# A decoder block with hybrid attention on one core: wait counts, the place of four weight chunks in the stream, and the shape of two row operations are changed

## The chip, the cores and the metric

The kernel runs on one core of one Trainium2 chip. The metric is device time in microseconds (us) of one execution, the median of several runs. The engines are named as the profile names them: PE is TensorE (matmuls; PEld its weight loads), DVE is VectorE, ACT is ScalarE, POOL is GpSimd and SP is SyncE, which here only issues DMAs. Each engine works through its own instructions in the order in which the program issues them. The program does not reorder them: the schedule is written by hand.

## The reference

One layer of a decoder block, batch 1, 256 tokens, model width 1024, float32. Cut to what matters:

```python
h = x @ w_in                                   # q, k, v, z, gates, NSA q and three k/v pairs
q, k, v = silu(causal_dwconv([dq, dk, dv]))    # 8 heads of 128, q and k l2-normalised
g = cumsum(log decay per chunk of 64)          # gated delta rule:
lower = strict_tril(k_beta @ k.T * decay)
u, w = triangular_solve(I + lower, [v_beta, k_beta * exp(g)])
for each chunk: v_new = u - w @ S; out = q_dec @ S + qk @ v_new; S = S * g_last + k_dec.T @ v_new
y_dn  = rmsnorm(out) * silu(z)
y_nsa = gates * (compressed + selected-block + window attention)   # 8 heads, 2 kv heads, rotary
y = sig(mg_dn) * (y_dn @ W_dn) + sig(mg_nsa) * (y_nsa @ W_nsa)
x = LN(alpha * x + y @ W_out)
x = LN(alpha * x + conv_glu(x))                # up (2 x 2816), causal conv of 3, silu gate, down
```

The output is x, 256 x 1024.

## The kernel before, in words

**The weight stream.** All big weights are cut into chunks of 128 x 1024 values. `plan()` (L66) writes the order in which they are stored and used: the input projection (k, q, kc, vc, nq, ksl, kwn, vt, and the 16 cmp chunks between them, then v, z, mgd, mgn), the two branch projections (wd, wn), the output projection (wo) and the feed-forward network: for each of 22 rounds a chunk ug (gate) and a chunk uv (value) of the up projection, in the rounds 1 to 15 also the chunk dn of the down projection of the round before, and at the end the last seven, dn15 to dn21 (TAIL = 7). SP's queue brings a chunk into one of six buffers `raw` (`dma_chunk` L168, `feed` L236). `split_chunk` (L178) makes two parts of it: ACT casts it to the matmul's type (`hi`, L192), DVE subtracts to get the rest (`lo`, L197), and POOL does a quarter of that subtraction for the early chunks. The pair goes into a ring of three pairs, or, for a few chunks, into a home of its own that `set_alt` names: dn15 and dn16 have theirs in the buffer YD, dn17 in `latemisc`, dn18 in `latev`. `ahead(limit, most)` (L222) splits the next chunks in the plan's order, at most `most` of them, as long as the ring has room; a chunk with a home of its own needs no room.

**The GEMMs.** `mm_feat` (L313) multiplies a chunk with the activations: 24 matmuls of 128x128 by 128x256 (lines L319 to L321: hi times hi, hi times lo, lo times hi) into a PSUM buffer of the tag "g", of which there are two. `feat` then lets an engine evacuate the result, calls `ahead` and calls `pump()` once.

**The side work.** Everything else (gates, the delta rule, compression, attention, norms of the heads) is written as generators. `pump` (L112) takes each living generator one step further, so that its instructions come behind those of the GEMM just issued. A generator gives way at a `yield`; `wait(name)` gives way as many times as the tables `W` and `WAITS` say, for the name and its running index. `back0`, for example, is the first wait called "back". These counts set behind which chunk's GEMM each piece of side work stands on all engines. Its PSUM comes from four buffers of the tag "s". Flags ("vcc", "vb", "levels" and so on) order the generators among one another.

The parts that the diff touches:
- `smalls` (L354 on): gates and decays from a small projection. `s1` stands before its exponentials, `pgm` before the matmuls of the cumulated decays.
- `delta` (L464 on): `ss` before the sums of squares go through the matmuls pss; then the row and column factors (lnr, rcat, bL), a transpose pr of the rows (L499), the rows' way through DRAM into `seed`; then on POOL the masks (L514, four operations, into KD), which add each mask to a factor; then `mask`, and for each of two matrices a shuffle (L519), an addition of its mask (L520) and an Exp on ACT. After the similarity matmuls come the block inverse on POOL, its way through DRAM (`tscr`), `back`, and `levels`: matmuls pa, pu, pt with updates L613, L623, L624. The scan over chunks (L642 on) follows once v is ready ("vb").
- `cmp_end` (L784 on): the compressed keys and values. For values it waits `vcc`, copies the hidden rows into `AT[:, 4096:4456]` on POOL (L820), multiplies (pc, L824) and splits the result into three parts with a row of ACT and DVE operations (L830 to L836); ca waits stand before the hidden matmuls phs (L792).
- `attention`: `soft` computes the scores psa (L881, L882), maxima (L885), exponentials and scales; `weigh` transposes the probabilities (ppt, L926; evacuated by L928 on DVE and L930 on ACT; and pptc, evacuated by L942), and multiplies with the values (poa). `wc` stands before each pair of transposes, `wv` amid the poa matmuls.
- `onorms` (L703 on): the gated norm of the delta rule's heads, with matmuls pot (L719), L721, a cast L723.
- `norm1` (L1210): the first LayerNorm's scaling of a row tile of 1024 columns, half on DVE (L1212), half on ACT, ahead of the transposes pxt (L1192).

**The feed-forward rounds** (L1286 on). Round j multiplies ug, evacuates it with the causal conv (ACT L146, DVE L351 twice), calls `ahead`, does the same for uv, applies Silu (ACT), the product (DVE L1305), the cast (ACT L1309) and the rest (DVE L1310), calls `ahead` a third time, and in the rounds 1 to 15 adds the down matmuls of the round before. From round 17 on each call of `ahead` splits one chunk at most. The last seven down chunks follow at the end (pdn, L1269 to L1271), then the second LayerNorm.

Of the kernel before, what the change touches and what calls it, by code (L numbers as in the profile page):

```python
# [9 lines left out]
AF = mybir.ActivationFunctionType  # L10
OP = mybir.AluOpType
# [7 lines left out]
NFF = FF // 128  # L19
NCMP = 15  # L20
# [27 lines left out]
CMP_GROUP = 4  # L48
CMP_SLOTS = 6
TAIL = 7  # L50
N_CA = CP["mL"][0]


# [12 lines left out]
def plan():  # L66
    seq = list(HEAD)
    for n in ("v", "z", "mgd", "mgn", "wd", "wn"):
        seq += [(n, i) for i in range(8)]
    seq += [("wo", i) for i in range(8)]  # L70
    for j in range(NFF):
        seq += [("ug", j), ("uv", j)]
        if 0 < j <= NFF - TAIL:
            seq.append(("dn", j - 1))
    seq += [("dn", NFF - TAIL + i) for i in range(TAIL)]
    return seq


PLAN = plan()
CMP = [i for i, b in enumerate(PLAN) if b[0] == "cmp"]  # L80
GEMM = [i for i, b in enumerate(PLAN) if b[0] != "cmp"]
W = dict(p40=1, pgm=2, later=2, rows=1, mask=5, expL=0, expQ=0, vs=2, inv=2, step=1, back=5, lev=1, la=1,
         lb=1, sa=2, sb=1, sc=1, ra=4, rb=3, rc=0, rd=0, lw=0, tw=0, rw=0, ca=2, cb=1, smalls=1, w40=2, t40=1, s1=0, s2=1, wa=1, wb=1,
         wc=0, sv=0, wv=0, lc=0, vcc=5, s3=1, s4=1, ss=0, z=0, on=0, oc=1, sim=1, vb=1, rest=0, zz=1)
WAITS = dict(back0=5, ca0=2, ca1=0, cb0=2, cb1=5, expL0=0, expQ0=1, la0=2, la2=1, la3=3, later0=0, later1=1,
             later3=2, lb0=1, lb1=2, lb2=2, lb3=0, lc0=0, lc1=0, lev0=3, mask0=3, oc0=2, oc1=1, oc2=0, oc3=0,
             on0=0, p400=2, pgm0=3, rb0=11, ra0=1, rest0=2, rows0=1, s10=0, s30=1, s32=1, s34=0, s36=8, s37=0, s41=2,
             s42=3, s43=2, sa2=2, sc0=1, sc2=1, sc3=1, sim0=2, sim2=0, sim3=0, ss0=2, step2=0, sv0=0, t400=1,
             vb0=3, w400=2, wa0=1, wa1=3, wa3=2, wa5=3, wa7=2, wb0=0, wb2=2, wc0=0, wc1=2, wc4=0, wc5=0, wc6=0,
             wv0=4, wv1=0, z0=1, zz0=1)  # L90
PUMPS = {}
WO_T = 3
POOL, POOL_END = 768, 20
# [6 lines left out]
class Body:  # L100
# [106 lines left out]
        self.alt[self.gemm_index(kind, idx)] = [mem[:, o:o + 1024] for o in (0, 1024)]  # L207

    def next_chunk(self, kind, idx):
        i = self.cur  # L210
        assert PLAN[GEMM[i]] == (kind, idx), (PLAN[GEMM[i]], kind, idx)
        self.cur += 1
        return self.sp.pop(i)

    def done_chunk(self, kind, idx):
        i = self.gemm_index(kind, idx)
# [247 lines left out]
    def delta(self):  # L464
        nc = self.nc
# [18 lines left out]
        Rk, Rq, bL = rc[:, 0:16], rc[:, 16:32], self.small(16, "bL")  # L484
# [9 lines left out]
        nc.vector.tensor_tensor(ce[:, 0:16], Rk, GL, op=OP.add)  # L494
        nc.vector.tensor_copy(ce[:, 16:32], self.lnb)
        self.act(ce, ce, AF.Exp)
        yield from self.wait("rows")
        pr = self.ps("pr")
        nc.tensor.transpose(pr[0:32, 0:128], rc, self.cp("ident"))  # L499
# [2 lines left out]
        scr = self.dram.tile([2, 32, 64], F32, name="rscr")  # L502
        seed = self.LT[:, 1024:3072]
        nc.gpsimd.dma_start(scr.rearrange("e u t -> u e t"), rrow.rearrange("u (e t) -> u e t", e=2))
        yield from self.wait("rw")
        for e in range(2):
            nc.gpsimd.dma_start(seed[64 * e:64 * e + 33:32], bass.AP(tensor=scr.tensor, offset=scr.offset + 2048 * e,
                                                                     ap=[[0, 2], [1, 2048]]))
        bc = lambda t, n, m: t[:, :, None].to_broadcast([128, n, m])
        kd = self.KD.rearrange("p u j -> p (u j)").rearrange("p (w u j) -> p w u j", w=2, u=16)  # L510
        for w, (m, b) in enumerate((("mL", bL), ("mQ", Rk))):
            for hf in range(2):
                us = slice(8 * hf, 8 * hf + 8)
                nc.gpsimd.tensor_tensor(kd[:, w, us], self.cp(m)[:, None, :].to_broadcast([128, 8, 64]),  # L514
                                        bc(b[:, us], 8, 64), op=OP.add)
        yield from self.wait("mask")
        for w, dst in enumerate((L, QKT)):
            flat = dst.rearrange("p u j -> p (u j)")
# [4 lines left out]
        for c in range(4):  # L523
            us = slice(4 * c, 4 * c + 4)
# [49 lines left out]
        for j in range(15):  # L574
            n, m = 15 - j, j + 1
            t = tmp[:, :n * m].rearrange("p (r c) -> p r c", r=n)
# [14 lines left out]
        for w, dst in ((1, TT), (0, T)):  # L591
            tc = vf[:, 256 * w:256 * w + 256].rearrange("p (u j) -> p u j", j=16)
            for b in range(4):
                o = dst[:, :, 16 * b:16 * b + 16]
# [189 lines left out]
    def cmp_end(self, w, hp):  # L784
        nc = self.nc
        n = 4 * NCMP
        hid = self.small(n, f"hid{w}")
        ex = self.small(n, f"hex{w}")
        yield from self.wait("ca")
        pf = self.ps("phs")[:, :n]  # L790
        for c in range(2):
            nc.tensor.matmul(pf[:, 30 * c:30 * c + 30], hp[:, 128 * c:128 * c + 128], self.cp("sel"),  # L792
                             start=True, stop=True)
        self.act(ex, pf, AF.Exp, scale=-1.0)
        nc.vector.tensor_scalar(ex, ex, 1.0, None, op0=OP.add)
        nc.vector.reciprocal(ex, ex)
        nc.vector.tensor_tensor(hid, pf, ex, op=OP.mult)
        yield from self.wait("cb")
        hv = hid.rearrange("p (c g n) -> p c g n", c=2, g=2)
        w2 = self.pp("w2").rearrange("p (w c d) -> p w c d", w=2, c=2)  # L800
        if w == 0:
            po = self.ps("pc2")
            pk = po[:, :30].rearrange("p (g n) -> p g n", g=2)
            for c in range(2):
                nc.tensor.matmul(pk, w2[:, 0, c], hv[:, c], start=(c == 0), stop=(c == 1))
            nc.vector.tensor_copy(self.KCC, pk)
            kt = self.KCC[0:32]
            sh = self.consts.tile([32, 2, NCMP], F32, name="shc")
            nc.vector.stream_shuffle(sh, kt, [(i + 16) % 32 for i in range(32)])
            for t, m in ((kt, "ccos"), (sh, "csin")):  # L810
                nc.vector.tensor_tensor(t, t, self.cp(m)[0:32][:, None, :].to_broadcast([32, 2, NCMP]), op=OP.mult)
            nc.vector.tensor_tensor(kt, kt, sh, op=OP.add)
        else:
            self.flags.add("cmp")
            yield from self.wait("vcc")
            po = self.ps("pc2")
            rows = 6 * NCMP
            h6 = self.AT[:, 4096:4456].rearrange("p (c g b n) -> p c g b n", c=2, g=2, b=6)
            for c in range(2):
                nc.gpsimd.tensor_copy(h6[:, c], hv[:, c][:, :, None, :].to_broadcast([128, 2, 6, NCMP]))  # L820
            pv = po[0:rows, :256]
            for g in range(2):
                for c in range(2):
                    nc.tensor.matmul(pv[:, 128 * g:128 * g + 128], h6[:, c, g].rearrange("p b n -> p (b n)"),  # L824
                                     w2[:, 1, c], start=(c == 0), stop=(c == 1))
            vh, vm = (self.PTC[0:rows, 256 * i:256 * i + 256] for i in range(2))
            out = self.VCC.rearrange("p g d -> p (g d)")
            rest = self.scr("vr")[0:rows, :256]
            part = self.cp("vm")[0:rows]
            nc.scalar.copy(vh, pv)  # L830
            nc.vector.tensor_tensor(rest, pv, vh, op=OP.subtract)
            nc.scalar.copy(vm, rest)
            self.act(out, vh, AF.Copy, scale=part[:, 0:1])
            nc.vector.scalar_tensor_tensor(out, vm, part[:, 1:2], out, op0=OP.mult, op1=OP.add)
            nc.vector.tensor_tensor(rest, rest, vm, op=OP.subtract)
            nc.vector.scalar_tensor_tensor(out, rest, part[:, 2:3], out, op0=OP.mult, op1=OP.add)  # L836
            self.flags.add("vcc")

    def attention(self):
        nc = self.nc  # L840
# [65 lines left out]
        def weigh(n):  # L906
            while f"soft{n}" not in self.flags:
                yield
            qt, g = divmod(n, 2)
# [10 lines left out]
            for i2 in range(2):  # L920
# [10 lines left out]
                else:  # L931
# [4 lines left out]
                    for b in range(2):  # L936
                        nc.scalar.copy(PT[:, 2 * b, 2 * i2:2 * i2 + 2], pt[:, b])
                if i2 == 1:
                    pt = self.ps("pptc")[0:6 * NCMP].rearrange("p (i q) -> p i q", i=4)
                    for i in range(4):  # L940
                        nc.tensor.transpose(pt[:, i], e6[:, i].rearrange("p b n -> p (b n)"), ident)
                    nc.scalar.copy(PTC.rearrange("p (i q) -> p i q", i=4), pt)  # L942
                yield from self.wait("wa", 4 * (qt + 1))
            po = self.psum.tile([128, 512], F32, name="poa", tag="c", bufs=1)
            while "vcc" not in self.flags:
                yield
            nc.tensor.matmul(po, self.VCC[:, g], PTC, start=True, stop=False)
            bs = range(4) if qt else (0, 2)
            for b in bs:
# [68 lines left out]
    def run(self):  # L1018
        nc, A = self.nc, self.A
# [126 lines left out]
        res = self.NQ.rearrange("p h t -> p (h t)").rearrange("p (t d) -> p t d", t=2)  # L1146
# [62 lines left out]

        def norm1(t):  # L1210
            rs, nm = stats1(t)
            nc.vector.tensor_scalar(res[:, t, :512], res[:, t, :512], rs, nm, op0=OP.mult, op1=OP.add)  # L1212
            self.act(res[:, t, 512:], res[:, t, 512:], AF.Identity, scale=rs, bias=nm)

        pg0 = [self.psum.tile([128, 512], F32, name="pg", tag=t, bufs=1)[:, :256] for t in "oc"]

# [43 lines left out]
        for i, home in enumerate([yd[:, :2048], yd[:, 2048:], *spare]):  # L1260
            self.set_alt("dn", NFF - TAIL + i, home)

# [23 lines left out]
        for j in range(NFF):  # L1286
            uu = []
            for w, n in enumerate(("ug", "uv")):
# [8 lines left out]
                c = w * NFF + j  # L1297
                u = self.scr(n)[:, :256]
# [67 lines left out]
        for sl, eng in ((slice(0, 640), nc.scalar), (slice(640, 1024), nc.sync)):  # L1366
            r = res[:, 1, sl]
# [141 lines left out]
```

## Time and profile before

| | us |
|---|---|
| median of 3 runs | 571.38 (570.38 to 572.04) |
| the profiled execution | 570.68 |
| its span | 568.9 |
| outside the span | 1.78 |
| PE busy | 554.0 (97%) |
| DVE busy | 394.4 (69%) |
| ACT busy | 308.2 (54%) |
| POOL busy | 115.0 (20%) |

The span runs from the first to the last instruction of the profiled execution. Busy times are of that one execution. The granted TensorE clock was 0.996 on average. The list of waits names an instruction that stood still, the line that it belongs to, and the instruction that released it; a timeline gives the start, the length, the engine, the line and the tiles of single instructions, with the idle time before them in brackets; a table of stretches gives each engine's busy time between two points.

### The profile page before, as it was taken

Reading aid. Unit: us, or ns where it says so; the run is one execution under the profiler, and the core shown is the slowest. Engines: PE = TensorE matmul, PEld = TensorE weight load, DVE = VectorE, ACT = ScalarE, POOL = GpSimd, SP = SyncE. Lnnn points to the kernel's source line nnn. Section 1 sums busy time; section 2 is a strip of 40 time slices with the busy share of each in tenths; the row PEclk is TensorE's granted clock in tenths of the full one; section 3 lists DMA queues with packets and bytes.
Section 4 is the critical chain, followed back from the end, with each engine's and each line's share of the span. In section 5 each row is a group of like instructions: output and inputs, shape, how many; then the busy total and the mean of one; then the engine's idle time right before and its main releaser. Section 6 shows DMA issues by size and latency. Waiting matters only on the chain.

```text
span 568.9 us, 11592 instructions
## 1 busy us (share of the span) xinstructions
PE 554.0 (97%) x4585; PEld 508.2 (89%) x4585; DVE 394.4 (69%) x681; ACT 308.2 (54%) x568; POOL 115.0 (20%) x160
## 2 busy tenths in 40 slices
PE   9999999999998999999999999999999999999994
PEld 6999999878997998878998898899999999999974
DVE  2788744867976654466658486878777777778884
ACT  4656654524484466463777344465655555556651
POOL 2466624018500330003001000078000000000003
PEclk9999999999999999999999999999999999999998
DMA  8985556575852232233354645635655555555501
GB/s 313 407 326 167 171 192 244 196 262 161 247 176 76 75 129 96 75 95 104 105 181 154 217 159 184 249 117 180 214 183 191 190 182 191 185 185 173 200 1 74
DMA packets 28182, 99.94 MB, mean 176 GB/s; under 512 B 3340, under 2 KB 3996, under 8 KB 27740
## 3 DMA queue, kind: packets, MB, share of 16 engines
q1 hardware_dynamic: 27312, 95.94, 49.5%
q0 software_dynamic: 672, 2.93, 1.7%
q8 instruction: 36, 0.59, 0.4%
q10 hardware_dynamic: 144, 0.33, 0.1%
q14 instruction: 18, 0.15, 0.1%
HBM read 97.33 MB, written 1.46 MB: 174 GB/s over the span
## 4 chain that ended last, share of the span: by engine, by line
PE 74%; DVE 8%; ACT 7%; DMA 4%; issue 3%; POOL 3%; SPq 0%; DVEq 0%; ACTq 0%; POOLq 0%
PE pg L319 16%; PE pg L321 16%; PE pg L320 16%; PE pdn L1270 3%; PE pdn L1271 3%; PE pdn L1269 3%; DVE lo L197 2%; ACT hi L192 2%; PE poa L951 2%; POOL VN L579 1%; PE pwo L994 1%; PE pwo L993 1%; PE pwo L992 1%; POOL itmp L577 1%; DMA VN<-tscr 1%
## 5 line engine op out<-in xcount | busy, mean ns | idle before, releaser
L197 DVE TENSOR_TENSOR lo<-raw,hi 128x1024 fp32r<-128x1024 f32 (+1 forms) x147 | 181.7, 1238 | 77.6 <-ACT hi L192 76.2
L192 ACT CAST hi<-raw 128x1024 fp32r<-128x1024 f32 (+1 forms) x151 | 154.7, 1029 | 34.3 <-PE pg L320 11.8
L319 PE MATMUL pg<-X,hi 128*128 128x256 f32 x496 | 143.7, 290 | 0.9 <-ACT V L1048 0.9
L320 PE MATMUL pg<-X,hi 128*128 128x256 f32 x496 | 139.7, 282 | 0.0
L321 PE MATMUL pg<-X,lo 128*128 128x256 f32 x496 | 139.6, 282 | 0.0
L319 PE MATMUL pg<-Y,hi 128*128 128x256 f32 x400 | 113.3, 283 | 0.0
L321 PE MATMUL pg<-Y,lo 128*128 128x256 f32 x400 | 112.6, 282 | 0.0
L320 PE MATMUL pg<-Y,hi 128*128 128x256 f32 x400 | 112.6, 282 | 0.0
L319 PEld LDWEIGHTS pg<-X,hi 128*128 128x128 f32 x496 | 93.5, 188 | 6.1 <-issue 3.1
L320 PEld LDWEIGHTS pg<-X,hi 128*128 128x128 f32 x496 | 93.5, 189 | 0.3 <-issue 0.2
L321 PEld LDWEIGHTS pg<-X,lo 128*128 128x128 f32 x496 | 93.5, 188 | 0.0
L320 PEld LDWEIGHTS pg<-Y,hi 128*128 128x128 f32 x400 | 75.4, 188 | 0.3 <-issue 0.2
L319 PEld LDWEIGHTS pg<-Y,hi 128*128 128x128 f32 x400 | 75.3, 188 | 0.2 <-issue 0.2
L321 PEld LDWEIGHTS pg<-Y,lo 128*128 128x128 f32 x400 | 75.3, 188 | 0.0
L1345 POOL TENSOR_TENSOR NQ<-NQ,AT 128x512 f32<-128x512 f32 x2 | 2.6, 1287 | 159.7 <-ACT NQ L146 159.7
L1270 PE MATMUL pdn<-lo,X 128*128 128x512 f32 (+1 forms) x90 | 31.6, 351 | 0.0
L1269 PE MATMUL pdn<-hi,X 128*128 128x512 f32 (+1 forms) x90 | 31.5, 350 | 0.0
L1271 PE MATMUL pdn<-hi,X 128*128 128x512 f32 (+1 forms) x90 | 31.4, 349 | 0.0
L902 POOL TENSOR_SCALAR AT<-AT,sums 128x128 f32<-128x128 f32 (+1 forms) x12 | 10.9, 918 | 89.3 <-DVE sums L894 46.8
L351 DVE SCALAR_TENSOR_TENSOR uv<-pg,ppk,uv 128x255 f32<-128x255 f32 (+1 forms) x44 | 21.2, 481 | 11.0 <-ACT uv L146 9.8
L351 DVE SCALAR_TENSOR_TENSOR cv<-pg,ppk,cv 128x255 f32<-128x255 f32 (+2 forms) x48 | 23.1, 481 | 8.1 <-ACT cv L146 6.9
L1309 ACT CAST X<-ug 128x256 fp32r<-128x256 f32 x22 | 9.0, 407 | 33.2 <-DVE ug L1305 33.2
(355 smaller groups left out, 943.9 us busy)
## 6 DMA issues: line engine op xcount, KB each, us to landing
raw<-in_w SPq DMA_DIRECT2D x156, 512.0 KB, 3.4
AT<-in_w SPq DMA_DIRECT2D x12, 512.0 KB, 6.3
Z<-in_w SPq DMA_DIRECT2D x4, 512.0 KB, 8.0
AT<-in_first SPq DMA_DIRECT2D x3, 512.0 KB, 6.3
V<-in_xk POOLq DMA_DIRECT2D x1, 1024.0 KB, 6.1
KD<-in_lnp POOLq DMA_DIRECT2D x1, 1024.0 KB, 5.0
AT<-in_lnp SPq DMA_DIRECT2D x1, 1024.0 KB, 8.4
AT<-in_first SPq DMA_DIRECT2D x2, 256.0 KB, 3.2
```

The source lines that it names most:

```text
L192: nc.scalar.copy(hi[:, o:o + n], raw[:, o:o + n])
L197: nc.vector.tensor_tensor(lo[:, :n], raw[:, :n], hi[:, :n].bitcast(F32), op=OP.subtract)
L319: nc.tensor.matmul(pg, hi[:, k], src[:, 0, k], start=(k == 0), stop=False)
L320: nc.tensor.matmul(pg, hi[:, k], src[:, 1, k], start=False, stop=False)
L321: nc.tensor.matmul(pg, lo[:, k], src[:, 0, k], start=False, stop=(k == 7))
L351: nc.vector.scalar_tensor_tensor(dst[:, s:], pg[:, :S - s], cw[:, n - 1 - s:n - s], dst[:, s:], op0=OP.mult, op1=OP.add)
L902: (nc.vector, nc.gpsimd)[b].tensor_scalar(e, e, w, None, op0=OP.mult)
L951: nc.tensor.matmul(po, self.VT[:, b % 2, c0:c0 + 128], PT[:, b].rearrange("p i q -> p (i q)"), start=False, stop=(b == bs[-1]))
L1269: nc.tensor.matmul(p, fh[:, ts], hi[:, sl], start=(j == 0), stop=False)
L1270: nc.tensor.matmul(p, fh[:, ts], lo[:, sl], start=False, stop=False)
L1271: nc.tensor.matmul(p, fl[:, ts], hi[:, sl], start=False, stop=(j == NFF - 1))
L1309: nc.scalar.copy(fh, f)
```

## The change

Five things are changed together.

1. LATE = 4: the chunks dn15 to dn18 move in the plan, and so in the stream, from behind uv21 to behind uv18, uv19, uv20 and uv21, one each. `next_chunk` takes a chunk by its name and no longer in the plan's order. The down matmuls stay where they were.
2. Wait counts: `vcc` 5 to 7, `back0` 5 to 6, `ca0` 2 to 3, `mask0` 3 to 4, `pgm0` 3 to 2, `s10` 0 to 1, `ss0` 2 to 1, `wc4` 0 to 1, `wv0` 4 to 3.
3. The four mask operations of `delta` move ahead: two before the wait "rows", two between the rows' DMA write and their read.
4. In `cmp_end` the copies on POOL stand before the wait `vcc` and go to another buffer, and the row of ACT and DVE operations is spread over three pumps; in `weigh` the flag "vcc" is awaited before pptc and no longer before poa.
5. `norm1` scales its row tile in quarters of 256 columns, two on DVE and two on ACT.

```diff
+LATE = 4
...
         if 0 < j <= NFF - TAIL:
             seq.append(("dn", j - 1))
-    seq += [("dn", NFF - TAIL + i) for i in range(TAIL)]
+        if NFF - LATE <= j:
+            seq.append(("dn", NFF - TAIL + j - NFF + LATE))
+    seq += [("dn", NFF - TAIL + i) for i in range(LATE, TAIL)]
...
     def next_chunk(self, kind, idx):
-        i = self.cur
-        assert PLAN[GEMM[i]] == (kind, idx), (PLAN[GEMM[i]], kind, idx)
         self.cur += 1
-        return self.sp.pop(i)
+        return self.sp.pop(self.gemm_index(kind, idx))
...
+        def masks(w, m, b):
+            for hf in range(2):
+                us = slice(8 * hf, 8 * hf + 8)
+                nc.gpsimd.tensor_tensor(kd[:, w, us], self.cp(m)[:, None, :].to_broadcast([128, 8, 64]),
+                                        bc(b[:, us], 8, 64), op=OP.add)
+        masks(0, "mL", bL)
         yield from self.wait("rows")
         pr = self.ps("pr")
...
         nc.gpsimd.dma_start(scr.rearrange("e u t -> u e t"), rrow.rearrange("u (e t) -> u e t", e=2))
+        masks(1, "mQ", Rk)
         yield from self.wait("rw")
         for e in range(2):
             nc.gpsimd.dma_start(seed[64 * e:64 * e + 33:32], ...)
-        for w, (m, b) in enumerate((("mL", bL), ("mQ", Rk))):
-            for hf in range(2):
-                us = slice(8 * hf, 8 * hf + 8)
-                nc.gpsimd.tensor_tensor(kd[:, w, us], ...)
         yield from self.wait("mask")
...
             self.flags.add("cmp")
+            h6 = self.misc[:, :360].rearrange("p (c g b n) -> p c g b n", c=2, g=2, b=6)
+            for c in range(2):
+                nc.gpsimd.tensor_copy(h6[:, c], hv[:, c][:, :, None, :].to_broadcast([128, 2, 6, NCMP]))
             yield from self.wait("vcc")
             po = self.ps("pc2")
             rows = 6 * NCMP
-            h6 = self.AT[:, 4096:4456].rearrange("p (c g b n) -> p c g b n", c=2, g=2, b=6)
-            for c in range(2):
-                nc.gpsimd.tensor_copy(h6[:, c], hv[:, c][:, :, None, :].to_broadcast([128, 2, 6, NCMP]))
...
             nc.vector.tensor_tensor(rest, pv, vh, op=OP.subtract)
+            yield
             nc.scalar.copy(vm, rest)
             self.act(out, vh, AF.Copy, scale=part[:, 0:1])
+            yield
             nc.vector.scalar_tensor_tensor(out, vm, part[:, 1:2], out, op0=OP.mult, op1=OP.add)
...
                 if i2 == 1:
+                    while "vcc" not in self.flags:
+                        yield
                     pt = self.ps("pptc")[0:6 * NCMP].rearrange("p (i q) -> p i q", i=4)
...
             po = self.psum.tile([128, 512], F32, name="poa", tag="c", bufs=1)
-            while "vcc" not in self.flags:
-                yield
...
             rs, nm = stats1(t)
-            nc.vector.tensor_scalar(res[:, t, :512], res[:, t, :512], rs, nm, op0=OP.mult, op1=OP.add)
-            self.act(res[:, t, 512:], res[:, t, 512:], AF.Identity, scale=rs, bias=nm)
+            for o in (0, 256):
+                r = res[:, t, o:o + 256]
+                nc.vector.tensor_scalar(r, r, rs, nm, op0=OP.mult, op1=OP.add)
+            for o in (512, 768):
+                r = res[:, t, o:o + 256]
+                self.act(r, r, AF.Identity, scale=rs, bias=nm)
```

More of the change, by code (lines that the diff above doesn't have):

```diff
@@ L83 @@
          lb=1, sa=2, sb=1, sc=1, ra=4, rb=3, rc=0, rd=0, lw=0, tw=0, rw=0, ca=2, cb=1, smalls=1, w40=2, t40=1, s1=0, s2=1, wa=1, wb=1,
[L84 to L90, printed above, removed]
+         wc=0, sv=0, wv=0, lc=0, vcc=7, s3=1, s4=1, ss=0, z=0, on=0, oc=1, sim=1, vb=1, rest=0, zz=1)
+WAITS = dict(back0=6, ca0=3, ca1=0, cb0=2, cb1=5, expL0=0, expQ0=1, la0=2, la2=1, la3=3, later0=0, later1=1,
+             later3=2, lb0=1, lb1=2, lb2=2, lb3=0, lc0=0, lc1=0, lev0=3, mask0=4, oc0=2, oc1=1, oc2=0, oc3=0,
+             on0=0, p400=2, pgm0=2, rb0=11, ra0=1, rest0=2, rows0=1, s10=1, s30=1, s32=1, s34=0, s36=8, s37=0, s41=2,
+             s42=3, s43=2, sa2=2, sc0=1, sc2=1, sc3=1, sim0=2, sim2=0, sim3=0, ss0=1, step2=0, sv0=0, t400=1,
+             vb0=3, w400=2, wa0=1, wa1=3, wa3=2, wa5=3, wa7=2, wb0=0, wb2=2, wc0=0, wc1=2, wc4=1, wc5=0, wc6=0,
+             wv0=3, wv1=0, z0=1, zz0=1)
 PUMPS = {}
@@ L496, in delta @@
         self.act(ce, ce, AF.Exp)
+        bc = lambda t, n, m: t[:, :, None].to_broadcast([128, n, m])
+        kd = self.KD.rearrange("p u j -> p (u j)").rearrange("p (w u j) -> p w u j", w=2, u=16)
+        def masks(w, m, b):
[4 more added lines that the diff above has]
+        masks(0, "mL", bL)
         yield from self.wait("rows")
@@ L508, in delta @@
                                                                      ap=[[0, 2], [1, 2048]]))
-        bc = lambda t, n, m: t[:, :, None].to_broadcast([128, n, m])
-        kd = self.KD.rearrange("p u j -> p (u j)").rearrange("p (w u j) -> p w u j", w=2, u=16)
-        for w, (m, b) in enumerate((("mL", bL), ("mQ", Rk))):
-            for hf in range(2):
-                us = slice(8 * hf, 8 * hf + 8)
-                nc.gpsimd.tensor_tensor(kd[:, w, us], self.cp(m)[:, None, :].to_broadcast([128, 8, 64]),
-                                        bc(b[:, us], 8, 64), op=OP.add)
         yield from self.wait("mask")
```

## The prediction

> **What bounds the kernel now.** I read the page first, then PE's waits, then stretches and single timelines where the diff acts.
>
> ```profile
> span 568.9 us, 11592 instructions
> PE 554.0 (97%) x4585; PEld 508.2 (89%) x4585; DVE 394.4 (69%) x681; ACT 308.2 (54%) x568; POOL 115.0 (20%) x160
> PE 74%; DVE 8%; ACT 7%; DMA 4%; issue 3%; POOL 3%; SPq 0%; DVEq 0%; ACTq 0%; POOLq 0%
> ```
>
> TensorE is busy 97% of the span and holds 74% of the chain. The diff neither adds nor removes a matmul, so it can only take away TensorE's waits or make new ones. These are the waits that the diff touches:
>
> ```profile
> PE psa L881 <- DVE LT L623: 2.1, 1, 2.1
> PE pg L319 <- ACT V L1048: 0.9, 1, 0.9
> ...
> PE ppt L926 <- ACT KD L146: 0.7, 1, 0.7
> ...
> PE phs L792 <- DVE LT L534: 0.5, 1, 0.5
> PE pdn L1270 <- DVE latev L197: 0.5, 1, 0.5
> PE pxt L1192 <- DVE NQ L1212: 0.4, 1, 0.4
> PE pr L499 <- DVE rcat L486: 0.4, 1, 0.4
> ```
>
> They add up to 5.5 us, so no more than about 1% can be won. What can be lost is read from the stages' balance: a middle FFN round with three chunks, a late one with two, and the stretch of the longest wait.
>
> ```profile
> core 0: us, PE busy (x) PEld busy (x) DVE busy (x) ACT busy (x) POOL busy (x), PEclk, DMA share, GB/s
> 468.90:477.40 8.50, 8.50 (x65) 8.11 (x64) 6.24 (x10) 4.67 (x7) 0.00 (x0) 1.00 0.57 189
> 523.27:528.97 5.70, 5.70 (x51) 5.70 (x49) 5.02 (x9) 3.63 (x6) 0.00 (x0) 1.00 0.53 184
> 171.00:174.40 3.40, 1.33 (x9) 0.78 (x7) 2.49 (x4) 1.13 (x2) 0.00 (x0) 1.00 0.06 18
> ```
>
> VectorE is busy 6.24 of 8.50 us in the middle round, but 5.02 of 5.70 in the late one.
>
> **The change, part by part.** The largest part is the plan. With LATE=4 the chunks of dn15 to dn18 stand behind uv18 to uv21, and they have homes of their own, so a split of one needs no place in the ring. Rounds 17 to 19 now split two chunks each: the third call of `ahead` finds the ring full. By the new order that call finds room in every one of them (uv18, dn15, ug19; uv19, dn16, ug20; uv20, dn17, ug21). The third split stands behind L1310 and ahead of the next round's evacuation of ug. Before's own trace shows that place empty and, once, filled, when round 20 splits dn16:
>
> ```profile
> 527.09 0.42 DVE L1310 TENSOR_TENSOR X<-ug,X 128x256 fp32r<-128x256 f32 x1 [0.47 <-ACT X L1309]
> 527.56 1.00 DVE L351 SCALAR_TENSOR_TENSOR ug<-pg,ppk,ug 128x255 f32<-128x255 f32 x2
> ...
> 538.49 0.43 DVE L1310 TENSOR_TENSOR X<-ug,X 128x256 fp32r<-128x256 f32 x1 [0.47 <-ACT X L1309]
> 539.44 1.23 DVE L197 TENSOR_TENSOR YD<-raw,YD 128x1024 fp32r<-128x1024 f32 x1 [0.52 <-ACT YD L192]
> 540.58 0.99 DVE L351 SCALAR_TENSOR_TENSOR ug<-pg,ppk,ug 128x255 f32<-128x255 f32 x2
> ```
>
> ```profile
> 528.97 0.28 PE L319 MATMUL pg<-Y,hi 128*128 128x256 f32 x1
> ```
>
> From L1310 to L351 it is 0.47 us empty and 2.09 filled: 1.62 later. At 540.58 that cost TensorE nothing, because only down matmuls followed. In rounds 17 to 19 another ug follows, two GEMMs later, in the same one of two PSUM buffers. L351 ends at 527.56 + 1.00 = 528.56 and that GEMM starts at 528.97, a slack of 0.41. So the first filled round makes TensorE wait 1.62 − 0.41 = 1.21. From then on VectorE sets the round: 5.02 busy, 0.47 for X's cast, 0.52 for the split's cast and 1.14 (540.58 − 539.44) make 7.15, 1.45 over 5.70, twice. Together 4.11, before ug19, ug20 and ug21. In return latev is split early and the tail's 0.5 goes. **+3.6.** Bounds: were VectorE's waits filled with other work, only 5.02 + 1.23 − 5.70 = 0.55 a round would be over, +1.1 in all; were all hidden, −0.5. I take the upper end, since the filled place is copied from the same kernel, and engines run in order.
>
> Next to it a rule: the Trainium skill ("Perfetto Trace Analysis", section "Optimization Strategy") says that bubbles that repeat on the busiest engine can mean too few buffers for the next tile. By it alone a third buffer would hide the three waits. The 7.15 against 5.70 speaks against that for more than a round.
>
> The masks (four L514 on POOL) move to either side of the row transpose pr. Three rows of the window from 96 to 102 us, and the page's row of all splits:
>
> ```profile
> L197 DVE TENSOR_TENSOR lo<-raw,hi 128x1024 fp32r<-128x1024 f32 x1 | 4.0, 3990 | 1.6 <-ACT hi L192 1.6
> L514 POOL TENSOR_TENSOR KD<-cpk,bL 128x512 f32<-128x512 f32 x2 | 2.1, 1064 | 0.0
> L514 POOL TENSOR_TENSOR KD<-cpk,rcat 128x512 f32<-128x512 f32 x2 | 2.1, 1046 | 0.0
> ```
>
> ```profile
> L197 DVE TENSOR_TENSOR lo<-raw,hi 128x1024 fp32r<-128x1024 f32 (+1 forms) x147 | 181.7, 1238 | 77.6 <-ACT hi L192 76.2
> ```
>
> ```profile
> 103.49 1.06 ACT L146 ACTIVATE LT<-LT 128x1024 f32<-128x1024 f32 x1 [6.66 <-DVE LT L520]
> 104.46 0.35 ACT L1046 COPY NQ<-pg 128x256 f32<-128x256 f32 x1
> 104.82 0.36 ACT L1048 COPY V<-pg 32x256 f32<-32x256 f32 x1
> ```
>
> Beside them a split took 3.99 instead of 1.24, so the shuffles and the Exp came 2.75 later, and the evacuation behind the Exp, which TensorE waited 0.9 for, with them. **−0.9** (0 to −1.0). At the new place a split of the same kind will be long by as much, once for each pair; it stands behind an evacuation that is done by then, so I cost it at nothing. Uncovered it would be up to 2.75, which I count as a rival's tail only. The masks queue ahead of the row DMAs on POOL; `mask0` at 4 keeps their pump.
>
> s1 comes a pump later, behind q7's Silu:
>
> ```profile
> 81.91 1.28 ACT L141 ACT_TABLE_LOAD   x1
> 83.20 0.29 ACT L146 ACTIVATE lnr<-pss,eps 128x32 f32<-128x32 f32 x1
> ```
>
> The Exp table is then in place when lnr comes, 1.28 earlier, and pr's 0.4 goes: **−0.4** (to +0.3, if pgm waits for POOL, which starts a pump later). phs is later by a pump: **−0.5**.
>
> `back0` puts the inverse's levels a chunk later, past two more of vcc's pumps. This removes psa's 2.1, which has its cause in these rows:
>
> ```profile
> 171.91 1.23 DVE L197 TENSOR_TENSOR lo<-raw,hi 128x1024 fp32r<-128x1024 f32 x1 [2.25 <-ACT hi L192]
> 173.05 0.68 DVE L623 TENSOR_TENSOR LT<-LT,pt 128x512 f32<-128x512 f32 x1
> ```
>
> But L623 and L624 then stand behind the next split in the same way, the two vcc steps and pv's eviction queue with the attention's exponentials, and the later psa waits in turn. A psa that meets VectorE one split late waits up to 1.23, and pa or pv that meet it an L623 late 0.68: 1.9 for the 2.1, too close to call a difference: **0** (−2.1, if no new wait comes, to +1.0, if both take place twice). The scan's start hangs on the flag "vb" and stays.
>
> `wc4` moves one pair of probability transposes, and with it pptc and the outputs, a pump later, into a pump with pot:
>
> ```profile
> 280.90 0.57 ACT L930 COPY AT<-ppt 128x512 f32<-128x512 f32 x1
> ...
> 283.02 0.62 ACT L723 CAST YD<-y 128x512 fp32r<-128x512 f32 x1 [1.07 <-DVE y L721]
> 283.54 0.37 ACT L1028 COPY LT<-pg 128x256 f32<-128x256 f32 x1
> 283.81 1.05 ACT L192 CAST hi<-raw 128x1024 fp32r<-128x1024 f32 x1
> ```
>
> ```profile
> 282.01 0.64 PE L719 MATMUL pot<-cpk,V 128*128 128x128 f32 x4
> 282.41 0.36 PE L319 MATMUL pg<-X,hi 128*128 128x256 f32 x1
> ```
>
> That pump now asks for five PSUM tiles of four banks. The last, the second pot, needs the bank of a ppt whose eviction L930 stands on ACT behind L723, L1028 and the cast L192. The cast ends at 284.86 now; the chain before it runs some 1.0 earlier (ppt's 0.7 and part of L930's 0.57), so 283.9. L930 takes it to 284.4, the pot's four matmuls to 284.85, against 282.41 for the next GEMM: **+2.4** (−0.7, if the bank is another, to +3).
>
> Norm rows in quarters:
>
> ```profile
> 372.54 0.55 DVE L1212 TENSOR_SCALAR NQ<-NQ,mv 128x512 f32<-128x512 f32 x1
> ```
>
> The first transposes need only a half of that row's work: **−0.2** (0 to −0.4).
>
> **Sum:** 3.6 − 0.9 − 0.4 − 0.5 + 0 + 2.4 − 0.2 = +4.0. On the profiled execution (570.68, of which 568.9 are span) it gives 574.7, on the median of the runs, 0.70 higher, 575.4; I put down 575.0, between them.
>
> **Rivals.**
> - *The forecast:* both queues bite. 575.0, and 573.4 to 577.0 with the bounds of single terms. 0.58.
> - *Late splits hide:* VectorE takes the third split in its 0.68 us of idle time a round and in the slack. For it: R20 does so without a wait. Against it: only downs follow there. 3.6 becomes −0.5: −0.1, 571.3. 0.12.
> - *The fifth tile finds a bank:* −0.7 for 2.4: +0.9, 572.3. 0.13.
> - *Side engines lag unfelt (the other side):* the tile that TensorE needs next always lies in a bank that was given back earlier. Its places are ug19 to ug21 and the pump after mgn5; it decides where L351 is late by less than the 0.41 of slack, and L930 by less than a pump. For it: TensorE is 97% busy with engines that are up to 2.75 late. It gives −0.9 − 0.4 − 0.5 − 0.2 − 0.7 − 0.5 = −3.2, 568.2. 0.14.
> - *The clock:* if a gap were long enough to lower it. In the row 171.00:174.40 TensorE was busy 1.33 of 3.40 us and PEclk stayed 1.00; my longest gap is 2.4. If the clock went to half for a stretch as long as that row's 3.40, it would add 1.7: 576.7. 0.03. The Trainium skill ("TensorE: Matmul & The Clock Gate", section "What's actually happening") gives an idle window of about 3.4 us before the clock is halved and as much busy time to get it back; the row stays below and agrees.
>
> **The numbers.** 0.3%, 1.7 us, is about what a measurement of this kernel can tell from no change. Faster: the fourth case and a part of the second with psa's wait gone, 0.18. Same: the second and third, 0.22. Slower: 0.60. The range of 569.7 to 577.0 leaves out the other side and a little above; the forecast's own is 573.4 to 577.0.
>
> **What would show it.** Three waits of 1.2 to 1.5 us of pg on L351 before ug19, ug20 and ug21, none of pdn on latev; one of about 2 us of pot on L930 near 283; no wait on L1048, phs or pr; psa's wait of 2.1 in smaller pieces. A late round of 5.7 us with a third split, or no wait behind mgn5, would prove me wrong.

## The result and the profile after

The changed kernel takes 577.85 us (median of 4 runs, 576.46 to 580.32), the kernel before 570.88 beside it: a ratio of 1.0123 (95% interval 1.0095 to 1.0152), 7.0 us slower. The forecast was +4.0 on the profiled execution, put down as 575.0 with a range up to 577.0: the direction was right, the size 3 us short.

The profiled execution took 580.32, 2.5 above the median. Its page begins:

```profile
span 578.5 us, 11600 instructions
## 1 busy us (share of the span) xinstructions
PE 556.3 (96%) x4585; PEld 509.5 (88%) x4585; DVE 393.8 (68%) x683; ACT 306.2 (53%) x568; POOL 113.6 (20%) x160
```

TensorE has the same 4585 matmuls, and the span is 9.6 longer. The list of TensorE's waits answers to the one of before (what waited, its line, what released it: us in total, times, the longest):

```profile
PE psa L887 <- DVE A L617: 3.7, 2, 2.6
PE pg L320 <- DVE ug L352: 3.5, 3, 1.2
PE pg L329 <- DMA AT<-in_first: 1.9, 1, 1.9
PE pot L723 <- ACT AT L936: 1.7, 1, 1.7
PE pv L552 <- ACT AT L149: 1.1, 1, 1.1
PE pw L290 <- PEq L1509: 0.8, 1, 0.8
PE po L693 <- ACT VN L676: 0.8, 1, 0.8
PE pxt L1198 <- DVE NQ L1220: 0.3, 1, 0.3
PE pa L615 <- DVE LT L628: 0.3, 1, 0.3
```

Set against the list of before, part by part: the head's three waits (pg on V 0.9, phs 0.5, pr 0.4) are gone, −1.8. In the z GEMMs psa's 2.1 has become 3.7 + 1.1 + 0.3 = 5.1, +3.0. In the attention's second half ppt's 0.7 has become pot's 1.7 and po's 0.8, +1.8. In the late rounds pdn's 0.5 has become 3.5, +3.0. The norm's 0.4 is 0.3. Together +5.9. The wait for the first activations, 1.9 against 0.5, is no part of the change: in the profiles of the kernels below, which leave the start alone as well, it lies anywhere from nothing to 2.0. Before the change the row was

```profile
PE pg L328 <- DMA AT<-in_first: 0.5, 1, 0.5
```

This profile is of the slowest of the four runs, and its psa waits are the largest with these levels: where only the plan's part or only the wc4 part is undone (below), psa, pv and pa add up to 3.4 and 3.8 instead of 5.1. So the z GEMMs' share is between +1.3 and +3.0, and all waits together between +4.2 and +5.9.

Here is a late round (from ug20's GEMM to ug21's) and the eight us behind pot's wait; PEclk is the clock that was granted to TensorE:

```profile
core 0: us, PE busy (x) PEld busy (x) DVE busy (x) ACT busy (x) POOL busy (x), PEclk, DMA share, GB/s
537.92:544.99 7.07, 5.93 (x49) 5.75 (x49) 6.00 (x10) 4.47 (x8) 0.00 (x0) 1.00 0.67 222
284.00:288.00 4.00, 2.24 (x15) 1.82 (x16) 2.79 (x4) 2.80 (x5) 0.06 (x1) 0.94 0.01 2
288.00:292.00 4.00, 4.00 (x25) 4.00 (x24) 2.63 (x5) 1.24 (x2) 0.56 (x1) 0.64 0.83 313
```

The late round takes 7.07 us; 7.15 was forecast. Behind pot's wait the clock falls: (0.06 + 0.36) x 4.00 = 1.7 us worth of clock is missing, and no wait shows it. With 5.9 and the 1.4 at the start that is 9.0 of the 9.6. Over all runs the clock is worth less than in this one: its mean is 0.9942 in the four runs of the change, and 0.9945 to 0.9956 in the series of the kernel before below, a difference worth 0.2 to 0.8 us.

### The profile page after: what moved, and what is told of

It reads as the page before. It is cut to its first block, busy times and chain, and to the rows that moved or that the text cites. A ratio compares the mean times of both kernels' runs of the same rounds, so it can differ in the third digit from the quotient of the medians.

```text
span 578.5 us, 11600 instructions
## 1 busy us (share of the span) xinstructions
PE 556.3 (96%) x4585; PEld 509.5 (88%) x4585; DVE 393.8 (68%) x683; ACT 306.2 (53%) x568; POOL 113.6 (20%) x160
## 4 chain that ended last, share of the span: by engine, by line
PE 51%; DVE 10%; ACT 8%; issue 2%; POOL 1%; POOLq 0%; DVEq 0%; ACTq 0%
PE pg L320 11%; PE pg L322 10%; PE pg L321 10%; DVE lo L200 3%; PE pdn L1280 3%; PE pdn L1279 3%; PE pdn L1281 3%; ACT hi L195 3%; PE poa L957 1%; PE pwo L1000 1%; PE pwo L999 1%; PE pwo L998 1%; ACT AT L149 1%; PE pg L1231 1%; ACT V L149 1%
## 5 line engine op out<-in xcount | busy, mean ns | idle before, releaser
L200 DVE TENSOR_TENSOR lo<-raw,hi 128x1024 fp32r<-128x1024 f32 (+1 forms) x147 | 179.0, 1219 | 80.7 <-ACT hi L195 79.4
L352 DVE SCALAR_TENSOR_TENSOR cv<-pg,ppk,cv 128x255 f32<-128x255 f32 (+2 forms) x48 | 23.1, 481 | 8.1 <-ACT cv L149 6.9
L352 DVE SCALAR_TENSOR_TENSOR uv<-pg,ppk,uv 128x255 f32<-128x255 f32 (+1 forms) x44 | 21.2, 481 | 10.7 <-ACT uv L149 9.8
```

The source lines that it names most:

```text
L200: nc.vector.tensor_tensor(lo[:, :n], raw[:, :n], hi[:, :n].bitcast(F32), op=OP.subtract)
L352: nc.vector.scalar_tensor_tensor(dst[:, s:], pg[:, :S - s], cw[:, n - 1 - s:n - s], dst[:, s:], op0=OP.mult, op1=OP.add)
```

## The experiments

All are timed against the kernel before on the same chip, which had medians of 571.03 to 571.53 there. Differences from the change are differences of the two ratios, times 571.

**One part undone at a time.** The first is the change with `LATE = 0`.

```diff
-LATE = 4
+LATE = 0
```

> The change without its plan part (LATE = 0). Theory: the three waits of pg on L352 (3.5 us together) are the plan's own and go, and the tail's wait on latev (0.5) comes back: about 3.3 below the change, so some +3.7 against the kernel before. Rival: VectorE is late there for other reasons and TensorE meets it elsewhere: less than 1 below the change.

Measured: 574.51, ratio 1.0053 (1.0033 to 1.0073), so (1.0123 − 1.0053) x 571 = 4.0 less than the change (3.3 was expected). The three waits are gone and the tail's is back, as forecast:

```profile
PE pdn L1280 <- DVE latev L200: 0.5, 1, 0.5
```

The plan's part is shown: 4 us, where 3.6 was forecast.

The second undoes the two counts that move the probability transposes.

```diff
-wc4=1 ... wv0=3
+wc4=0 ... wv0=4
```

> The change with wc4 and wv0 as before (0 and 4). Theory: pot's wait on L936 (1.7) and po's (0.8) go, ppt's 0.7 comes back: about 2.1 below the change, and 1.5 more where the clock fell behind pot's wait, so +3.5 to +4.9 against the kernel before, and the granted clock stays at 1.00 between 284 and 292 us. Rival: the crowded pump only moves and another tile waits for its bank: about the time of the change, and the clock falls all the same.

Measured: 574.34, 1.0062 (1.0039 to 1.0084), 3.5 less than the change. Its clock is 1.00 in all stretches from 276 to 300 us. pot's wait and po's are gone and ppt's 0.7 is back, as the theory said. In the change, pot's wait reads as forecast, on ACT and then on PE:

```profile
284.61 0.62 ACT L727 CAST YD<-y 128x512 fp32r<-128x512 f32 x1 [1.54 <-DVE y L725]
285.13 0.37 ACT L1034 COPY LT<-pg 128x256 f32<-128x256 f32 x1
285.40 1.05 ACT L195 CAST hi<-raw 128x1024 fp32r<-128x1024 f32 x1
286.34 0.59 ACT L936 COPY AT<-ppt 128x512 f32<-128x512 f32 x1
```

```profile
286.99 0.66 PE L723 MATMUL pot<-cpk,V 128*128 128x128 f32 x4 [1.70 <-ACT AT L936]
```

The eviction that frees the bank stands last in ACT's queue behind a weight chunk's cast. The waits explain 1.8 of the 3.5. The mean clock of the runs, 0.9952 against 0.9942, is worth some 0.5 more; the remaining 1.2 is no more than the two intervals leave open.

The third lets the levels start where they did before.

```diff
-back0=6
+back0=5
```

> The change with back0 = 5 alone put back. Theory: the levels' first product of pa (L617) stands again ahead of the split that waits for the Silu of v, the 5.7 us of new waits (psa on L617 twice, pv, pa) go and psa's 2.1 of before returns: about 3.5 below the change, +3.5 against the kernel before. Rival: the new waits come from the compressed values' part (vcc = 7 and the two extra yields), which stays: about the time of the change.

Measured: 578.15, 1.0128 (1.0100 to 1.0157): no gain. The theory fell. The rival's time came but not its reason, since none of the waits that it means is left; others stand in their place (the second fence has the columns of the late round above):

```profile
PE pg L320 <- DVE Z L352: 2.4, 1, 2.4
...
PE pa L615 <- ACT LT L149: 1.4, 1, 1.4
```

```profile
160.00:164.00 4.00, 1.55 (x27) 1.45 (x23) 3.10 (x6) 3.84 (x7) 0.00 (x0) 0.62 0.00 0
164.00:168.00 4.00, 4.00 (x21) 4.00 (x21) 3.19 (x6) 2.87 (x2) 0.00 (x0) 0.53 0.43 148
```

pa now waits for the copies of the inverse itself: the inverse is late. And behind this gap, too, the clock falls to about half, in a profile that is of the slowest of the six runs; two of the six have a mean clock of 0.987 and 0.988, the other four 0.994 to 0.995.

**All three undone.** This leaves the head, the compressed values' part and the norm.

```diff
-LATE = 4 ... back0=6 ... wc4=1 ... wv0=3
+LATE = 0 ... back0=5 ... wc4=0 ... wv0=4
```

> The change without the plan part, with wc4, wv0 and back0 as before. Theory: what is left are the gains of the head (masks, s1, ca0: 2.3) and of the norm's quarters (0.15): 2.5 below the kernel before, ratio 0.9957. Rival: the head's gains are given back in the z GEMMs, where the scan's start is tied to the flag vb: equal to the kernel before.

Measured: 572.34 (12 runs), 1.0012 (0.9994 to 1.0030): no gain at all. The gain is given back in the z GEMMs, as the rival says, but not at the scan's start: pa waits 1.1 for the inverse and the next GEMM 1.6 for Z behind it. (The profile is of the fastest of the 12 runs, 569.34 us with a mean clock of 0.995; the mean over the 12 is 0.9919.) The inverse starts when its blocks have made a trip through DRAM (written to `lscr`, read back into VN). POOL's timeline shows the trip, first of the kernel before, then of this one:

```profile
120.70 1.24 POOL L567 DMA_DIRECT2D lscr<-VN  x1 [20.95 <-DVE hex L795]
125.45 0.57 POOL L569 DMA_DIRECT2D VN<-lscr  x1 [3.51 <-PE pc L805]
128.66 0.22 POOL L577 TENSOR_TENSOR itmp<-VN 128x15 f32<-128x15 f32 x1 [2.63 <-DMA VN<-lscr]
```

```profile
119.62 1.23 POOL L571 DMA_DIRECT2D lscr<-VN  x1 [26.18 <-DVE VN L576]
125.82 0.58 POOL L573 DMA_DIRECT2D VN<-lscr  x1 [4.97 <-DMA lscr<-VN]
131.42 0.53 POOL L581 TENSOR_TENSOR itmp<-VN 128x15 f32<-128x15 f32 x1 [5.02 <-DMA VN<-lscr]
```

The write is issued 1.1 earlier, but the inverse starts 2.8 later: 131.42 − 119.62 = 11.8 us instead of 128.66 − 120.70 = 8.0. TensorE, meanwhile, is earlier: it would have started the first pa at 158.31 − 1.10 = 157.21 and not at 159.06:

```profile
159.06 1.15 PE L611 MATMUL pa<-LT 64*64 64x64 f32 x32
```

```profile
158.31 1.15 PE L615 MATMUL pa<-LT 64*64 64x64 f32 x32 [1.10 <-ACT LT L149]
```

The trip's length is no accident of one run. It is 11.9 (131.85 − 120.00) in the change itself and 11.6 to 11.8 in the eight other profiles that have the new head and the transfers as they were, and 7.9 to 8.1 in the four with the old head. So a new theory: the head's gain is eaten by this trip, and the gaps that follow cost clock on top.

**The trip left out.** The inverse does not read its blocks back.

```diff
-nc.gpsimd.dma_start(vf[:, 256:512], sl.rearrange(...))
+nc.gpsimd.memset(vf[:, 256:512], 0.0)
```

> The kernel of the run before (no plan part, wc4, wv0 and back0 as before) with one thing left out: the diagonal blocks are not read back from DRAM, the inverse works on zeros that POOL writes in their place. Theory: the head's gain is lost in this trip through DRAM (write and read took 5.8 and 5.4 us to land after the change, 4.2 and 3.1 before it), so the inverse comes too late for the levels; without the trip pa's wait (1.1), that of the GEMM behind it on Z (1.6) and the drop of the clock go: 567.5 to 569.5, ratio about 0.995. Rival: the levels wait for VectorE's order, not for the inverse: 572, as with the trip.

Measured: 566.40, 0.9909 (0.9891 to 0.9927), 5.9 below the same kernel with the trip, and more than the theory allowed (567.5 to 569.5). The two waits (2.7) and the mean clock (0.9960 against 0.9919, 2.3) account for 5.0 of it. The list of waits has nothing left between the start and the attention:

```profile
PE pg L329 <- DMA AT<-in_first: 2.0, 1, 2.0
PE pw L290 <- PEq L1509: 0.8, 1, 0.8
PE ppt L932 <- ACT KD L149: 0.7, 1, 0.7
PE pdn L1280 <- DVE latev L200: 0.5, 1, 0.5
PE pxt L1198 <- DVE NQ L1220: 0.3, 1, 0.3
```

So the inverse's arrival is what the levels wait for, and not only VectorE's order. The edit takes away the wait for the whole trip, not only the 3.8 that it grew by: POOL finishes the inverse some 10 us earlier (the write to `tscr` is issued at 138.10 instead of 148.34). What a trip of the old length would give was not tried.

**The gap filled, with the trip.**

```diff
+if first: self.fill(8)     # 128x256 bf16 matmuls into an unused tile
 for i, u, r in tiles(us): nc.tensor.matmul(pa[r, i], ...)
+if first: self.fill(12)
```

> The same kernel as the one above, with the trip, plus 8 and 12 small matmuls on TensorE (about 0.9 and 1.3 us, into an unused PSUM tile) just before and behind the first pa, where TensorE waits 1.1 and 1.6 us. They do no work of the computation. Theory: these gaps lower the clock in most runs (mean granted clock 0.992 in twelve runs, 0.995 in the fastest), and TensorE kept busy holds it: clock 0.995 or more, some 1.5 us faster, 570.5. Rival: only the gaps' own length counts: no gain, 572 to 573.

Measured: 570.20 (12 runs), 0.9979 (0.9966 to 0.9992), 2.1 less than without the fillers. The GEMM behind still waits 2.0 for Z in its profile. The mean granted clock over the runs is 0.9963, against 0.9919 without fillers: 0.0044 x 570 = 2.5 us. Matmuls that compute nothing made the kernel faster, and the clock accounts for it: the theory holds here.

**The Silu later.**

```diff
-sv0=0
+sv0=1
```

> The change with the Silu of v one pump later (sv0 = 1). Theory: psa waits 2.6 at 167 us because L617 stands behind the split of a chunk whose cast stands behind the table load and the Silu (1.28 + 1.92 us); a pump later it doesn't: that wait goes, 2.5 below the change, +4.5 against the kernel before, less what v's later arrival costs the scan. Rival: L617 is late because the inverse is late: psa's wait stays, about the time of the change.

Measured: 579.65, 1.0140 (1.0115 to 1.0165), not to be told from the change: the theory fell, and the time is the rival's. psa still waits 3.4, now on another operation (L878) and in two pieces, and pa waits 1.1 and then 3.8. In the change itself psa's first wait reads so on ACT and DVE:

```profile
164.20 1.92 ACT L149 ACTIVATE V<-Z 128x2048 f32<-128x2048 f32 x1
166.15 0.37 ACT L1106 COPY Z<-pg 128x256 f32<-128x256 f32 x1
166.42 1.05 ACT L195 CAST hi<-raw 128x1024 fp32r<-128x1024 f32 x1
```

```profile
167.50 1.23 DVE L200 TENSOR_TENSOR lo<-raw,hi 128x1024 fp32r<-128x1024 f32 x1 [2.86 <-ACT hi L195]
168.64 0.69 DVE L617 TENSOR_TENSOR A<-pa,cpk 128x512 f32<-128x512 f32 x1
```

L617 is in the queue behind a split that waits 2.86 for ACT. The chain is there, but to move the Silu alone is no cure.

**The levels' part alone**, on the kernel before (`back0` 6, `vcc` 7, the compressed values' part, the flag's place):

```diff
-vcc=5 ... back0=5
+vcc=7 ... back0=6
```

> The kernel before with the levels' part of the change alone (back0 6, vcc 7, the compressed values' part, the flag's new place). Theory: a chunk later the first L617 stands behind the split that waits for the Silu of v, whether the inverse is late or not: waits of psa as in the change (3.5 for 2.1), +1 to +3. Rival, the prediction's own price: old waits go, new ones of the same size come, 0.

Measured: 571.09 (12 runs), 1.0003 (0.9991 to 1.0016): the rival, the prediction's own price of 0. Its waits are those that the prediction counted (1.7 for the 2.1):

```profile
PE psa L883 <- DVE A L613: 1.0, 1, 1.0
...
PE pv L548 <- ACT AT L146: 0.5, 1, 0.5
...
PE pa L611 <- DVE LT L624: 0.2, 1, 0.2
```

By itself the term was right. It is wrong only together with the earlier head. The difference is to be seen on ACT, first in the change, then with the levels' part alone:

```profile
160.69 0.91 ACT L149 ACTIVATE LT<-VN,cpk 128x256 f32<-128x256 f32 x2 [2.10 <-DMA VN<-tscr]
```

```profile
158.35 1.71 ACT L146 ACTIVATE LT<-VN,cpk 128x256 f32<-128x256 f32 x4
162.76 1.91 ACT L146 ACTIVATE V<-Z 128x2048 f32<-128x2048 f32 x1
```

These copies of the inverse stand ahead of the Silu of v. In the change ACT stands still for 2.10 us until the inverse is back from its second trip through DRAM (`tscr`), and the Silu starts at 164.20 instead of 162.76, although TensorE issues the first pa 2.2 us earlier (160.38 instead of 162.62). With the levels' part alone the copies wait for nothing. So the late inverse reaches psa with back0 = 6 too, by way of ACT's queue; this is read from the traces, and no run moves it alone.

**Why is the trip longer?** A kernel without the three parts that issues no weight transfers for some pumps around the trip:

```diff
 def feed(self):
+    if self.hold: return      # set behind the second similarity block, until the inverse's first pump
```

> The kernel without the plan part and with wc4, wv0 and back0 as before, and with no weight transfer issued from the third block of similarities until the inverse's first pump (some three pumps). Theory: the trip through DRAM is slow because the weights' transfers are in flight beside it; held back, write and read land in about 4 and 3 us as in the kernel before, the inverse starts some 3 us earlier, pa's and Z's waits shrink or go: 568 to 570 (0.994 to 0.998 of the kernel before), against 572.3 with the trip as it is. Rival: the trip's length is that of its small pieces: it stays at 11 us, 572; or the held weights come too late and TensorE waits for them: over 573.

Measured: 571.39 (12 runs), 0.9996 (0.9976 to 1.0016). The read landed in 2.5 us, the write in 6.8; the trip took 131.16 − 121.17 = 10.0 instead of 11.8, and the GEMM behind pa still waited 3.2 for Z. The gain, 0.9 by the ratios, lies inside the intervals, and the inverse started hardly earlier (131.16 against 131.42): neither the theory's trip of 7 us nor the rival's of 11. What was already in flight lay beside the write: while it ran, the DMA engines moved 256 GB/s, against 173 without the hold and 55 in the kernel before, and it took 6.8, 5.7 and 4.2 us. Beside the read they moved 226, 314 and 293 GB/s, and it took 2.5, 5.5 and 3.1. The lengths follow the traffic, but no run sets the traffic and nothing else. With dn15 to dn18 behind rounds 12 to 15 as well:

> The same with dn15 to dn18 behind rounds 12 to 15 instead of at the end, no fillers. Theory: 0.7 less than the run with held weights: 567.5 to 569.5. Rival: as there, plus or minus nothing.

Measured: 571.49 (12 runs from 566.68 to 572.44), 0.9982 (0.9958 to 1.0005): the rival, no gain. Its runs with a mean clock of 0.994 or more took 566.7 to 571.1, those below it 571.5 to 572.4.

**A third buffer in the late rounds.**

```diff
+if self.n_g is not None and self.n_g % 3 == 0:
+    return self.psum.tile([128, 512], F32, name="pg", tag="c", bufs=1)[:, :256]
```

> The change with a third PSUM buffer for the GEMMs from round 17 on (every third one takes the buffer of another tag). Theory: VectorE's round is longer than TensorE's, so a third buffer only puts the wait off by one GEMM (2.85 us): of the three waits (3.5 together) the first two go and about 0.6 to 1.2 of the last is left; some 2.5 below the change, +4.5 against the kernel before. Rival: the waits are a lack of buffers alone: all three go, +3.5, and no wait of pg on L352 is left.

> The change with a third PSUM buffer for the GEMMs from round 17 on, once more, for its profile. Theory (VectorE's round is the longer one): the waits of pg on L352 shrink from three to one of about 0.6 to 1.2 us. Rival (buffers alone): none is left.

Measured: 577.44 and 577.28, ratios 1.0095 (1.0067 to 1.0124) and 1.0092 (1.0062 to 1.0122). The execution profiled in the first took 1907.26 us, and its profile is not read here. In the second, no wait on L352 is left, but this one is new:

```profile
PE pg L328 <- DVE lo L206: 1.5, 2, 0.8
```

TensorE now waits for the split of the chunk that it is to multiply. Both expectations named the wrong wait; 1.5 of 3.5 stay, so the buffers were some of it; that VectorE's time is the rest is argued from its 6.00 busy of 7.07 us. In time the gain, some 1.8 us by the ratios, lies inside the intervals. The Trainium skill's rule on repeating bubbles ("Perfetto Trace Analysis", section "Optimization Strategy") fits the 2.0 that went, and not the 1.5.

**Better versions.** The late chunks where VectorE has room, on the kernel before with the norm in quarters:

```diff
+if 12 <= j < 16:
+    seq.append(("dn", NFF - TAIL + j - 12))
```

> The kernel before with the four chunks dn15 to dn18 behind the rounds 12 to 15 in the plan, where VectorE is busy 6.24 of 8.50 us, and with the norm in quarters. Theory: the splits cost nothing there, the tail's wait on latev (0.5) and 0.15 at the norm go: 0.7 below the kernel before, ratio 0.9988. Rival: the third split holds up ug's evacuation as it does in rounds 17 to 19: up to 1.2 a round, +1 to +4.

Measured: 570.49 (12 runs), 0.9984 (0.9968 to 1.0001); pdn's wait is gone, and no wait of the GEMMs on L351 comes in those rounds. With the head, the fillers and these late chunks:

> The kernel with the fillers around the first pa, and dn15 to dn18 behind rounds 12 to 15 instead of at the end (16 fillers behind pa instead of 12). Theory: the gains add up: 1.1 + 0.7 below the kernel before, 569.6, mean clock 0.996. Rival: the late chunks' gain of 0.5 lies inside the run's scatter: 570.4 as without it.

Measured: 569.61, 0.9966 (0.9954 to 0.9978): faster than both kernels, and the sum that the theory gave. Its interval overlaps that of the fillers alone (0.9966 to 0.9992), so the late chunks' own share is not shown. And the kernel before with late chunks, norm and fillers at psa's wait:

> The kernel before with the norm in quarters, dn15 to dn18 behind rounds 12 to 15, and 18 filler matmuls (some 2.0 us) just before the psa that waits 2.1 us at 172. Theory: the clock holds (mean 0.996 instead of 0.994): 0.9 + 1.2 below the kernel before, 569.2. Rival: in this stretch the clock does not fall, or the fillers come late and add to the wait: 570.5 to 572.

Measured: 570.33 (12 runs), 0.9982 (0.9964 to 0.9999), no more than without these fillers, although the mean clock is 0.9957 against 0.9939. So fillers gained in one gap and not in another.

## Why the prediction was right and wrong

- **Late chunks, +3.6: right.** Three waits on L352 before ug19, ug20 and ug21, of 1.21, 1.14 and 1.14 us, a round of 7.07 for the 7.15, and 4.0 by the run without LATE.
- **The masks −0.9, s1 −0.4, phs −0.5: right as waits in the change's profile, not as time.** All three waits are gone there (the first, on V, is back at 0.6 and 0.8 in the profiles with back0 = 5 and with held weights). No split beside the masks' old place is long any more, nor is one at their new place, where the prediction had expected it; two small VectorE operations beside the first pair of masks (L493, L496) took 0.89 and 1.03 us instead of 0.18 and 0.17:

```profile
L200 DVE TENSOR_TENSOR lo<-raw,hi 128x1024 fp32r<-128x1024 f32 x5 | 6.1, 1225 | 8.3 <-ACT hi L195 8.3
```

- **The levels, 0: this step failed.** The sum set old waits against new ones at the z GEMMs (bounds −2.1 to +1.0) and so took the inverse's arrival as given. Alone, the part costs nothing (1.0003). But the sum added it to a head that is 1.8 earlier, and the inverse, which lies between the two, did not come earlier: its trip through DRAM took 3.8 longer. The levels then meet the late inverse directly (pa, back0 = 5) or through ACT's queue (psa, back0 = 6): 2.7 to 5.1 us of waits for 2.1, where "smaller pieces" were forecast. The description of the kernel names the inverse on POOL and its way through DRAM; the sum prices neither. Head, levels and norm were to give −2.0; without the two other parts, and with back0 = 5, they measure +0.7 (1.0012, 0.9994 to 1.0030). That is 2.7 of the miss.
- **The crowded pump, +2.4: right in mechanism, too small.** pot waits for L936 as described. The waits grow by 1.8, but the part costs 3.5.
- **The clock, 0.03: its chance was too low.** It was made a rival because one gap of the profile kept 1.00. The change's profile shows 1.7 us lost behind a gap of 1.7, which is the rival's price. It belonged into the sum, beside the wait of pot that it follows, instead of among the rivals. Over all runs it is worth less (0.2 to 0.8 us).
- **The norm, −0.2:** 0.1 less wait; not tried alone.

By times, the parts come to 4.0 + 3.5 + 0.7 = 8.2 where 7.0 was measured; each has an interval of 1 to 2 us. What stays open is why the trip through DRAM is longer. The transfers beside it are a candidate that the run with held weights neither showed nor excluded.

## What to carry to other kernels

Here a gain ahead of a long side chain (DRAM trips, POOL) was worth nothing to what waits for the chain's end, because the chain itself did not come earlier: follow the chain from the moved step to its next reader before adding terms. Price a wait with the clock that it may cost, and look at the granted clock of many runs, not of one profile. Extra work for an engine belongs in stages where it has idle time: the same four splits cost 4.0 from round 17 on, and in rounds 12 to 15 nothing that was measured (0.9984, 0.9968 to 1.0001, with the norm in quarters).

## What the runs showed of the hardware

Gaps of TensorE lowered the granted clock in some places and not in others, and their length alone does not tell which. Behind pot's 1.7 it fell in all four profiles that have this wait. Behind pa's 1.4 and the next GEMM's 2.4 it fell to 0.53 (back0 = 5), behind 1.1 and 1.6 in the same places it did not (the profile with all three undone). In the change, the stretch with psa's wait of 2.6 kept it:

```profile
core 0: us, PE busy (x), PEclk, DMA share, GB/s
164.00:168.00 4.00, 2.73 (x24) 1.00 0.38 131
168.00:172.00 4.00, 2.62 (x19) 1.00 0.39 131
```

In the runs of the kernel before beside the first four experiments, the six with a mean clock of 0.997 took 569.3 to 571.3 us and the six with 0.992 took 570.9 to 573.8, so part of a kernel's scatter goes with its clock. TensorE need not be wholly idle for the clock to fall: in 284.00:288.00 it was busy 2.24 of 4.00 us and the clock then fell to 0.64. The Trainium skill ("TensorE: Matmul & The Clock Gate", section "What's actually happening") tells of a free-running window of about 3.4 us whose phase varies by run; the scatter agrees with it. By its table the clock is halved after an idle window; here the longest gaps in two stretches where it fell were 1.7 us (pot's, in the change) and 2.4 us (with back0 = 5). Whether the transposes and the 64x64 matmuls that ran beside these gaps count as work for the clock, no run here shows.
